# Half of the down projection's columns by Strassen's seven products, in a tuned encoder block

## The chip, the cores and the metric

The kernel runs on one core of a Trainium2 chip. Its time is the device time of one execution in microseconds, the median of a few runs; beside it stands one profiled execution. The engines are TensorE (PE; PEld is its load of the stationary operand), VectorE (DVE), ScalarE (ACT), GpSimd (POOL), and SyncE (SP), which here issues the DMAs. A matmul multiplies a stationary block (at most 128x128) by moving columns (at most 512) into a bank of PSUM, of which there are eight.

## The reference

One layer of an encoder on 256 tokens and 16 meta tokens, width 2048, all in float32. What matters here is its last part:

```python
def conv_glu(x, w_gate, w_up, conv_w, conv_b, w_down):
    g = x @ w_gate                     # 2048 -> 5632
    u = x @ w_up
    ...
    return (jax.nn.silu(gc) * u) @ w_down      # 5632 -> 2048

mix = jnp.concatenate([rmsnorm(out_a, ...), rmsnorm(out_b, ...)], axis=-1)
h = h + mix @ w_out[l]
h = h + conv_glu(rmsnorm(h, ffn_norm_g[l]), w_gate[l], w_up[l], conv_w[l], conv_b[l], w_down[l])
return h[:, N_META:]                   # (1, 256, 2048)
```

Ahead of it stand the input projection and two groups of attention heads, which the change leaves alone.

## The kernel before

**Layout and precision.** Activations are kept transposed, features on the 128 partitions and tokens along the free axis. Each float32 operand is split into two values of TensorE's rounded float32 type, hi (a copy by ACT) and lo (the value minus hi, by DVE). A product is made of three matmuls: hi by hi, hi by lo, lo by hi. The weights are the stationary operand. Where a tile holds hi and lo of the activations side by side (256 tokens each), `mm2` does the block in two matmuls: the weight's hi by 512 moving columns (L1433), the weight's lo by the 256 of hi (L1434). The two halves of the bank are added when it is evacuated. `mm3` (L398 to L400) takes three of 256 to 272 columns.

**Weights.** They come as parts of 128x1024 (eight blocks) or less. The list `pieces` sets the order in which they are loaded into five `raw` buffers, split by `split_hi` and `split_lo` into three buffers `whi` and three `wlo` (ACT L215, DVE L219, 512 columns at a time), and used by TensorE. A part's hi and lo buffers come free when TensorE is through with it.

**Stages.** Attention; output projection `w_out`; per pair of row chunks g (22 of them) the gate and up projections with their gating (`gated`), which leaves `act[:, f]`, 128 features of the 5632 with hi and lo; then the down projection: for each of the 16 output chunks m, 44 blocks f, `mm2` for the first 15 and `mm3` for the last, evacuated by `down_out` with the residual `hT[m]`, stored to `outT`.

**What sets the order.** The kernel is written as threads of steps. A planner, `Flow`, gives each step a cost and always records next the step that can start first. So the order on each engine's queue is fixed when the program is built, by those costs; on the chip every queue runs in this order, and a semaphore holds an instruction (and all behind it on its engine) until what it needs is there. The DMA issues on SP are ordered in the same way. `split_hi` and `split_lo` come ahead of other steps only when fewer than two parts are ready.

Of the kernel before, what the change touches and what calls it, by code (L numbers as in the profile page):

```python
# [15 lines left out]
P = 128  # L16
# [19 lines left out]
FC = D_FF // P  # L36

# [145 lines left out]
def encoder_block(ctx: ExitStack, tc: tile.TileContext, io):  # L183
# [101 lines left out]
    his = Slots(tiles(wpool, 3, [P, PW], "whi", F32R))  # L285
    los = Slots(tiles(wpool, 3, [P, PW], "wlo", F32R))
# [8 lines left out]

    pieces = []

# [30 lines left out]
    for m in range(KC):  # L328
        add(io["w_down"][m])

# [12 lines left out]
    def load_piece():  # L343
        p = pieces[n_loads[0]]
        n_loads[0] += 1
        p.raw = yield from one(raws)
        yield "sp", 600
        load(p.raw[:, : p.n], p.src, p.loaded, nc.sync)

# [17 lines left out]
    def split_lo():  # L367
        for p in pieces:
            p.lo = yield from one(los)
            for t, ev, ready in zip(p.parts, p.half, p.ready):  # L370
                yield ev
                yield from TT(p.lo[:, t], p.raw[:, t], p.hi[:, t].bitcast(F32), ALU.subtract)
                fl.set(ready)
            n_split[1] += 1
            fl.put(raws, p.raw)
# [38 lines left out]
    def const(name, n=P):  # L414
# [6 lines left out]
        t[:, :, :L] for t in tiles(hpool, KC, [P, 2, HW], "hl", F32R)  # L421
    ]

# [840 lines left out]

    def project(tiles, n, slots=acc):
# [10 lines left out]
    def attention_weights():  # L1276
# [74 lines left out]
        for parts, evs, evac in ((ob, ev_ob, out_b), (oa, ev_oa, out_a)):  # L1351
            for g in range(8):
# [7 lines left out]
                for c in range(2):  # L1360
                    fl.spawn(evac(2 * g + c, pss[c]))
        fl.spawn(scale_h())
# [6 lines left out]
    act = mts = None  # L1369

    def mlp_buffers():

        nonlocal act, mts
        yield ev_s2
        actx.close()
        mpool = ctx.enter_context(tc.tile_pool(name="mpool", bufs=1))
        act = mpool.tile([P, FC, 2, SEQ], F32R, name="act")
        mts = Slots(tiles(mpool, 6, [P, NT], "mt"))
# [4 lines left out]
    def gated(f, gate, up):  # L1383
# [27 lines left out]
        fl.put(mts, gc)  # L1411
        fl.set(ev_act[f])

    def down_out(m, ps):
        o = yield from one(mts)
        o_ = o[:, :SEQ]
        yield from TT(o_, ps[:, :SEQ], hT[m][:, :SEQ], ALU.add)
        if m < KC - 1:
            yield from TT(o_, ps[:, SEQ:], o_, ALU.add)
        fl.put(acc, ps)  # L1420
# [19 lines left out]
    def mlp_weights():  # L1440
        for g in range(FC // 2):
            pss = []
            for which, mul in enumerate((mm_gate, mm_up)):
                for _ in range(2):
                    pss.append((yield from one(acc)))
                for k in range(KC):
                    for c in range(2):
                        yield from mul(pss[2 * which + c], k)
            for c in range(2):
                fl.spawn(gated(2 * g + c, pss[c], pss[2 + c]))  # L1450
        for m in range(KC):
            ps = yield from one(acc)
            for f in range(FC):
                yield ev_act[f]
                if m < KC - 1:
# [5 lines left out]
            fl.spawn(down_out(m, ps))  # L1461
# [40 lines left out]
def _layout(inputs):  # L1502
# [42 lines left out]
    out["w_down"] = _columns(L0["w_down"], FC, 1)  # L1545
# [76 lines left out]
```

## Time and profile before

| what | value |
|---|---|
| time, median of 3 runs | 1132.37 us (1132.12 to 1132.48) |
| the profiled execution | 1132.44 us, of which the trace's span is 1130.7 |
| TensorE busy | 1125.1 us |
| VectorE busy | 809.6 us |
| ScalarE busy | 660.3 us |
| GpSimd busy | 122.2 us |
| moved by DMA | 203.62 MB, 180 GB/s over the span |

The span is the time from the trace's first to its last record. Busy time is the time in which an engine has at least one instruction under way. Matmuls overlap in the records, so that TensorE's pace is read from the distance between the starts of two of them.

### The profile page before, as it was taken

Reading aid. Unit: us, or ns where it says so; the run is one execution under the profiler, and the core shown is the slowest. Engines: PE = TensorE matmul, PEld = TensorE weight load, DVE = VectorE, ACT = ScalarE, POOL = GpSimd, SP = SyncE. Lnnn points to the kernel's source line nnn. Section 1 sums busy time; section 2 is a strip of 40 time slices with the busy share of each in tenths; the row PEclk is TensorE's granted clock in tenths of the full one; section 3 lists DMA queues with packets and bytes.
Section 4 is the critical chain, followed back from the end, with each engine's and each line's share of the span. In section 5 each row is a group of like instructions: output and inputs, shape, how many; then the busy total and the mean of one; then the engine's idle time right before and its main releaser. Section 6 shows DMA issues by size and latency. Waiting matters only on the chain.

```text
span 1130.7 us, 21889 instructions
## 1 busy us (share of the span) xinstructions
PE 1125.1 (100%) x8072; PEld 1062.2 (94%) x8072; DVE 809.6 (72%) x1685; ACT 660.3 (58%) x1466; POOL 122.2 (11%) x198
## 2 busy tenths in 40 slices
PE   9999999999999999999999999999999999999998
PEld 9999999999999999999999999999999888888888
DVE  8888888888878867766777677766776655555553
ACT  8787879797646655555555555555555544444442
POOL 0010212121332200100010001000100000000000
PEclk9999999999999999999999999999999999999999
DMA  9453534344655555555555555555555666676662
GB/s 347 152 171 114 163 128 142 129 145 148 208 187 185 185 186 188 177 192 186 188 177 191 185 189 181 187 187 187 185 186 187 181 195 192 208 209 197 192 196 72
DMA packets 62627, 203.62 MB, mean 180 GB/s; under 512 B 6840, under 2 KB 11448, under 8 KB 62520
## 3 DMA queue, kind: packets, MB, share of 16 engines
q1 hardware_dynamic: 62232, 201.97, 55.4%
q8 instruction: 63, 1.03, 0.4%
q14 instruction: 44, 0.36, 0.1%
q10 hardware_dynamic: 288, 0.26, 0.1%
HBM read 200.10 MB, written 2.10 MB: 179 GB/s over the span
## 4 chain that ended last, share of the span: by engine, by line
PE 97%; ACT 2%; DMA 0%; DVE 0%; POOL 0%; issue 0%; SPq 0%; POOLq 0%
PE bank L1433 28%; PE bank L398 16%; PE bank L399 16%; PE bank L400 16%; PE bank L1434 14%; PE bank L255 4%; PE bank L261 2%; ACT whi L215 1%; ACT scr L215 1%; DMA pt<-in_xT 0%; ACT bank L215 0%; ACT mq L215 0%; DVE scr L227 0%; ACT qraw L215 0%; POOL sq8r L243 0%
## 5 line engine op out<-in xcount | busy, mean ns | idle before, releaser
L219 DVE TENSOR_TENSOR wlo<-raw,whi 128x512 fp32r<-128x512 f32 (+1 forms) x737 | 512.5, 705 | 263.7 <-ACT whi L215 260.8
L215 ACT ACTIVATE whi<-raw 128x512 fp32r<-128x512 f32 (+1 forms) x737 | 459.0, 629 | 399.5 <-PE bank L1433 182.4
L398 PE MATMUL bank<-hl,whi 128*128 128x258 f32 (+1 forms) x1232 | 355.9, 289 | 0.2
L399 PE MATMUL bank<-hl,whi 128*128 128x258 f32 (+1 forms) x1232 | 351.2, 285 | 0.2 <-DVE hl L227 0.2
L400 PE MATMUL bank<-hl,wlo 128*128 128x258 f32 (+1 forms) x1232 | 349.2, 283 | 0.0
L1433 PE MATMUL bank<-hl,whi 128*128 128x512 f32 x704 | 246.3, 392 | 0.0
L400 PEld LDWEIGHTS bank<-hl,wlo 128*128 128x128 f32 x1232 | 234.9, 191 | 0.1
L399 PEld LDWEIGHTS bank<-hl,whi 128*128 128x128 f32 x1232 | 233.8, 190 | 0.7 <-DVE hl L227 0.3
L398 PEld LDWEIGHTS bank<-hl,whi 128*128 128x128 f32 x1232 | 232.4, 189 | 1.9 <-ACT whi L215 0.4
L1433 PE MATMUL bank<-act,whi 128*128 128x512 f32 x660 | 228.8, 391 | 0.0
L1434 PE MATMUL bank<-hl,wlo 128*128 128x256 f32 x704 | 197.5, 281 | 0.0
L1434 PE MATMUL bank<-act,wlo 128*128 128x256 f32 x660 | 184.8, 280 | 0.0
L1433 PEld LDWEIGHTS bank<-hl,whi 128*128 128x128 f32 x704 | 132.0, 188 | 28.9
L1433 PEld LDWEIGHTS bank<-act,whi 128*128 128x128 f32 x660 | 123.4, 187 | 27.1
L1434 PEld LDWEIGHTS bank<-hl,wlo 128*128 128x128 f32 x704 | 132.7, 188 | 0.0
L1434 PEld LDWEIGHTS bank<-act,wlo 128*128 128x128 f32 x660 | 124.7, 189 | 0.0
L243 POOL TENSOR_TENSOR mt<-mt,s 128x256 f32<-128x256 f32 x44 | 41.5, 964 | 459.6 <-ACT mt L215 459.6
L227 DVE SCALAR_TENSOR_TENSOR mt<-mt,vecs,mt 128x256 f32<-128x256 f32 x88 | 40.2, 478 | 0.0
L398 PE MATMUL bank<-ob,whi 128*128 128x258 f32 x128 | 36.8, 288 | 0.0
L399 PE MATMUL bank<-ob,whi 128*128 128x258 f32 x128 | 36.5, 285 | 0.0
L400 PE MATMUL bank<-ob,wlo 128*128 128x258 f32 x128 | 36.1, 282 | 0.0
L215 ACT ACTIVATE scr<-scr 128x272 f32<-128x272 f32 x68 | 28.1, 425 | 4.5 <-DVE scr L227 4.0
(211 smaller groups left out, 1207.8 us busy)
## 6 DMA issues: line engine op xcount, KB each, us to landing
raw<-in_w_gate SPq DMA_DIRECT2D x88, 512.0 KB, 4.4
raw<-in_w_up SPq DMA_DIRECT2D x88, 512.0 KB, 4.5
raw<-in_w_down SPq DMA_DIRECT2D x80, 512.0 KB, 4.4
raw<-in_w_in SPq DMA_DIRECT2D x54, 512.0 KB, 3.9
raw<-in_w_out SPq DMA_DIRECT2D x32, 512.0 KB, 4.0
raw<-in_w_down SPq DMA_DIRECT2D x16, 256.0 KB, 3.4
raw<-in_w_cq SPq DMA_DIRECT2D x5, 512.0 KB, 6.1
bias<-in_na_bias SPq DMA_DIRECT2D x8, 272.0 KB, 4.5
```

Source lines behind the costliest of these rows:

```text
L215: nc.scalar.activation(out, in_, f, **kw)
L219: nc.vector.tensor_tensor(out, a, b, op)
L227: nc.vector.scalar_tensor_tensor(out, a, s, b, op0, op1)
L243: nc.gpsimd.tensor_tensor(out, a, b, op)
L255: nc.tensor.matmul(o, l, r, start=start, stop=stop)
L261: nc.tensor.transpose(o, i, ident[:n, :n])
L398: nc.tensor.matmul(ps, whi, xhi, start=start, stop=False)
L399: nc.tensor.matmul(ps, whi, xlo, start=False, stop=False)
L400: nc.tensor.matmul(ps, wlo, xhi, start=False, stop=stop)
L1433: nc.tensor.matmul(ps, whi, x, start=start, stop=False)
L1434: nc.tensor.matmul(ps[:, :n], wlo, x[:, 0, :], start=False, stop=stop)
```

## The change

**Which columns.** The first 1024 of the 2048 output columns are no longer computed in the transposed layout but as tokens by columns, by Strassen's scheme (the variant with seven products and sums that are used again): the activations are cut in halves of 128 tokens and, per row pair g, of 128 features (chunks 2g and 2g+1); the weights of the pair in halves of 128 rows and 512 columns. Each product is 128 tokens by 512 columns, with the activations as the stationary and the weights as the moving operand, as three matmuls (hi by hi, hi by lo, lo by hi). Seven banks of PSUM collect the seven products over the 22 row pairs. The other 1024 columns stay on the plain path, in one bank.

**Sums of the activations.** `value_sums` makes four 128x128 sums per pair after the gating, splits them and stores them to DRAM; `load_pair` brings them back in the down stage (tiles `sin`).

**Sums of the weights.** A pair's four weight quarters are loaded as 1 MB into one of two `quarters` tiles; `weight_sums` makes three sums on DVE, one 1024 and two 512 wide. The four parts of a pair, A (1024 columns: two quarters), B (512: one quarter), C and D (1024 each: two sums each), are split into hi and lo like other parts; 3584 columns are split per pair, where the plain path would split 2048. The tiles take the space of `hl`, which comes free at the end of the last up projection.

**Order.** Parts of the scheme and of the plain chunks alternate: three plain parts, then two scheme parts and one plain, four scheme parts where a new plain chunk begins, and eight plain parts at the end.

**Around it.** The residual of the first eight chunks is transposed on TensorE after the output projection (`residual_transposed`, 16 transposes). `scheme_out` combines the seven products after the last pair, adds the residual on POOL and stores to `out`. `down_out` of the plain chunks evacuates by two copies on ACT, adds the residual on POOL and the second half on DVE. There are four instead of three buffers `whi` and `wlo`, and a smaller reserve for DMA descriptors of POOL, which starts no DMAs here.

The diff, cut to its core:

```diff
+SF = 1024
+ST = SF // P
+AHEAD, BEHIND = 3, 8
...
     raws = Slots(tiles(wpool, 5, [P, PW], "raw"))
-    his = Slots(tiles(wpool, 3, [P, PW], "whi", F32R))
-    los = Slots(tiles(wpool, 3, [P, PW], "wlo", F32R))
+    his = Slots(tiles(wpool, 4, [P, PW], "whi", F32R))
+    los = Slots(tiles(wpool, 4, [P, PW], "wlo", F32R))
...
+    scheme = [(r, p) for r in row_pairs for p in r.pieces]
+    n = len(others) - BEHIND
+    down += others[:AHEAD]
+    for i in range(AHEAD, n):
+        k = 4 if others[i - 1][0] != others[i][0] else 2
+        down += scheme[:k] + [others[i]]
+        del scheme[:k]
+    down += scheme + others[n:]
...
+    def load_pair(r):
+        r.raw = yield from one(quarters)
+        t = r.raw
+        for i in range(2):
+            yield "sp", 600
+            ev = r.loaded if i else Event()
+            load(t[:, i * PW : (i + 1) * PW], io["w_down_s"][r.g][:, i * PW : (i + 1) * PW], ev, nc.sync)
...
+        r.S = yield from one(s_parts)
+        yield s_saved[r.g]
+        yield "sp", 600
+        load(r.S, s_dram[r.g], r.ev_S, nc.sync)
+        fl.spawn(weight_sums(r), 2)
...
+    def weight_sums(r):
+        yield r.loaded
+        r.sums = yield from one(sums4)
+        t, raw, h = r.sums, r.raw, PW // 2
+        yield from TT(t[:, :PW], raw[:, h : 3 * h], raw[:, :PW], ALU.subtract)
...
+        yield from TT(t[:, PW : PW + h], raw[:, PW : PW + h], t[:, :h], ALU.subtract)
+        yield from TT(t[:, PW + h :], t[:, PW : PW + h], raw[:, PW + h :], ALU.subtract)
...
+    def residual_transposed():
+        for i in range(ST // 2):
+            for c in range(2):
+                yield ev_sqh[2 * i + c]
+            pt = yield from one(tps)
+            yield from TR(
+                [(pt[:, (2 * t + c) * P : (2 * t + c + 1) * P], hT[2 * i + c][:, t * P : (t + 1) * P])
+                 for t in range(2) for c in range(2)]
+            )
...
+    def value_sums(g, a, b):
...
+        yield from TT(S[0], A21, A22, ALU.add)
+        yield from TT(S[1], S[0], A11, ALU.subtract)
+        yield from TT(S[2], A11, A21, ALU.subtract)
+        yield from TT(S[3], A12, S[1], ALU.subtract)
...
+        yield from split_plain(parts[:, : PW // 2], parts[:, PW // 2 :], s)
+        yield "sp", 600
+        load(s_dram[g], parts.bitcast(F32), s_saved[g], nc.sync)
...
+        if m < KC - ST - 1:
+            t = yield from one(mts)
+            yield from ACT(o_, ps[:, :SEQ], AF.Copy)
+            yield from ACT(t[:, :SEQ], ps[:, SEQ:], AF.Copy)
+            fl.put(acc, ps)
+            yield from PTT(o_, o_, hT[ST + m][:, :SEQ], ALU.add)
+            yield from TT(o_, t[:, :SEQ], o_, ALU.add)
...
+    PRODUCTS = {"A": (3, 2), "B": (1,), "C": (5, 7), "D": (6, 4)}
...
+    def scheme_products(p, r):
...
+            yield from block()
+            t = slice(i * PW // 2, (i + 1) * PW // 2)
+            first, last = f == 0, f == FC - 2
+            yield from MM(
+                product3(sums7[n], a, (p.hi[:, t], p.lo[:, t]), first, last)
+            )
...
+    def scheme_out():
...
+        yield from ACT(c1, sums7[1], AF.Copy)
+        fl.put(acc, sums7[1])
+        yield from TT(C[0][0], sums7[2], c1, ALU.add)
...
-    nc = _bacc.Bacc("TRN2", target_bir_lowering=False, num_devices=1)
+    nc = _bacc.Bacc("TRN2", target_bir_lowering=False, num_devices=1, dynamic_dma_scratch_size=1024)
```

How it moves DVE's queue, at a place in the middle of the down projection. Before, `wlo` are the lo parts of the weights, and `mt` with `res` is an evacuation of a chunk with its residual:

```order
L219 TENSOR_TENSOR wlo_89<-raw_80,whi_86 128x512 x2
L219 TENSOR_TENSOR wlo_90<-raw_81,whi_87 128x512 x2
L219 TENSOR_TENSOR wlo_88<-raw_82,whi_85 128x512
L219 TENSOR_TENSOR wlo_89<-raw_83,whi_86 128x512 x2
L219 TENSOR_TENSOR wlo_90<-raw_84,whi_87 128x512 x2
L219 TENSOR_TENSOR mt_5198<-bank_72,res_3966 128x256
L219 TENSOR_TENSOR wlo_88<-raw_80,whi_85 128x512
L219 TENSOR_TENSOR mt_5198<-bank_72,mt_5198 128x256
```

Now, on the same engine and stage; L231 is the same helper. A `quarters` tile that is written is a pair's tile of weight sums, and `wlo` that reads one is a split of a scheme part:

```order
L231 TENSOR_TENSOR wlo_92<-quarters_10215,whi_88 128x512 x2
L231 TENSOR_TENSOR quarters_10191<-quarters_10141 128x1024
L231 TENSOR_TENSOR wlo_89<-quarters_10215,whi_85 128x512 x2
L231 TENSOR_TENSOR wlo_90<-raw_80,whi_86 128x512 x2
L231 TENSOR_TENSOR mt_5230<-mt_5231,mt_5230 128x256
L231 TENSOR_TENSOR wlo_91<-quarters_10141,whi_87 128x512 x2
L231 TENSOR_TENSOR wlo_92<-quarters_10141,whi_88 128x512
L231 TENSOR_TENSOR wlo_89<-raw_81,whi_85 128x512 x2
L231 TENSOR_TENSOR quarters_10191<-quarters_10141,quarters_10191 128x512
L231 TENSOR_TENSOR quarters_10191<-quarters_10191,quarters_10141 128x512
L231 TENSOR_TENSOR wlo_90<-quarters_10191,whi_86 128x512 x2
L231 TENSOR_TENSOR wlo_91<-quarters_10191,whi_87 128x512 x2
```

Between two plain parts there now stand splits of scheme parts and weight sums; the first sum of the next pair stands ahead of the split of this pair's D.

The queue of SP in the same stage, before, with what each issue waits for (DMAHW are the DMAs issued earlier):

```order
L338 DMA raw_82<-in_w_down 128x1024 [waits DMAHW7_49,DMAHW1_49,DVE_49]
L338 DMA raw_83<-in_w_down 128x1024 [waits DMAHW2_49,DVE_49]
L338 DMA raw_84<-in_w_down 128x1024 [waits DMAHW3_49,DVE_49]
L338 DMA raw_80<-in_w_down 128x1024 [waits DMAHW4_49,DVE_49]
L338 DMA raw_81<-in_w_down 128x512 [waits DMAHW5_49,DVE_49]
L1422 DMA outT<-mt_5199 128x256 [waits DVE_49]
```

Now, where `sin` is the load of a pair's activation sums and `quarters` that of its weights:

```order
L391 DMA raw_84<-in_w_down 128x1024 [waits DMAHW3_49]
L391 DMA quarters_10166<-in_w_down_s 128x1024 [waits DMAHW4_49,Activation_49]
L391 DMA quarters_10166<-in_w_down_s 128x1024 [waits DMAHW5_49]
L391 DMA sin_5241<-s_dram_114 128x1024 [waits DMAHW6_49,PE_49]
L391 DMA raw_80<-in_w_down 128x1024 [waits DMAHW7_49]
L391 DMA raw_81<-in_w_down 128x512 [waits DMAHW0_49,Activation_49]
L391 DMA quarters_10141<-in_w_down_s 128x1024 [waits DMAHW1_49,DVE_49]
L391 DMA quarters_10141<-in_w_down_s 128x1024 [waits DMAHW2_49,DVE_49]
L391 DMA sin_5240<-s_dram_115 128x1024 [waits DMAHW3_49,PE_49]
```

The weight loads now share the queue with loads of quarters, which wait for DVE and ACT, and with loads of activation sums, which wait for TensorE.

## Rows read from the trace of the kernel before

**Rows 1.** The page's parts 1 and 2: busy times, and TensorE by slices.
```profile
span 1130.7 us, 21889 instructions
PE 1125.1 (100%) x8072; PEld 1062.2 (94%) x8072; DVE 809.6 (72%) x1685; ACT 660.3 (58%) x1466; POOL 122.2 (11%) x198
...
PE   9999999999999999999999999999999999999998
...
PEclk9999999999999999999999999999999999999999
```

**Rows 2.** Busy time by stretch: early, gate and up, down.
```profile
core 0: us, PE busy (x) PEld busy (x) DVE busy (x) ACT busy (x) POOL busy (x), PEclk, DMA share, GB/s
10.00:15.00 5.00, 5.00 (x42) 4.91 (x41) 4.64 (x10) 4.45 (x11) 0.00 (x0) 1.00 1.04 416
...
30.00:40.00 10.00, 10.00 (x81) 10.00 (x81) 9.72 (x23) 7.26 (x18) 0.00 (x0) 1.00 0.42 134
395.00:883.00 488.00, 488.00 (x3424) 458.27 (x3423) 343.47 (x685) 255.52 (x471) 39.60 (x42) 1.00 0.57 185
885.00:1111.00 226.00, 226.00 (x1306) 199.27 (x1305) 123.46 (x200) 102.75 (x168) 1.90 (x2) 1.00 0.65 198
```

**Rows 3.** Groups from 880 to 1130 us: count, busy us, mean ns, idle before.
```profile
L1433 PE MATMUL bank<-act,whi 128*128 128x512 f32 x660 | 228.8, 391 | 0.0
L1434 PE MATMUL bank<-act,wlo 128*128 128x256 f32 x660 | 184.8, 280 | 0.0
```

**Rows 4.** Timeline of PE, down projection's first blocks and last chunk: start, length.
```profile
882.56 0.39 PE L1433 MATMUL bank<-act,whi 128*128 128x512 f32 x1
882.79 0.28 PE L1434 MATMUL bank<-act,wlo 128*128 128x256 f32 x1
882.90 0.39 PE L1433 MATMUL bank<-act,whi 128*128 128x512 f32 x1
...
1111.36 0.28 PE L398 MATMUL bank<-act,whi 128*128 128x256 f32 x1
...
1127.06 0.28 PE L400 MATMUL bank<-act,wlo 128*128 128x256 f32 x1
```

**Rows 5.** Timeline of PE in attention: six transposes (L261) and what follows.
```profile
229.54 0.82 PE L261 MATMUL bank<-consts,p 128*128 128x128 f32 x6
230.12 0.36 PE L398 MATMUL bank<-late,whi 128*128 128x258 f32 x1
230.32 0.28 PE L399 MATMUL bank<-late,whi 128*128 128x258 f32 x1
230.43 0.29 PE L400 MATMUL bank<-late,wlo 128*128 128x258 f32 x1
```

**Rows 6.** Timelines of POOL (first row) and DVE beside and behind it.
```profile
886.43 1.90 POOL L243 TENSOR_TENSOR mt<-mt,s 128x256 f32<-128x256 f32 x2 [20.72 <-ACT mt L215]
...
887.00 0.72 DVE L219 TENSOR_TENSOR wlo<-raw,whi 128x512 fp32r<-128x512 f32 x1
887.64 0.41 DVE L219 TENSOR_TENSOR mt<-bank,mt 128x256 f32<-128x256 f32 x1
...
888.52 1.28 DVE L219 TENSOR_TENSOR wlo<-raw,whi 128x512 fp32r<-128x512 f32 x2
889.73 0.41 DVE L219 TENSOR_TENSOR act<-mt,act 128x256 fp32r<-128x256 f32 x1
890.07 0.41 DVE L219 TENSOR_TENSOR mt<-mt,mt 128x256 f32<-128x256 f32 x1
```

**Rows 7.** DMA issues (count, KB, us to landing), and SP's longest wait (total, times, longest).
```profile
raw<-in_w_down SPq DMA_DIRECT2D x80, 512.0 KB, 4.4
...
SPq L338 <- DVE wlo L219: 767.2, 316, 6.7
```

**Rows 8.** Waits of TensorE's weight loads for a weight part (total, times, longest).
```profile
PEld bank L398 <- ACT whi L215: 0.4, 1, 0.4
```

More of the change, by code (lines that the diff above doesn't have):

```diff
@@ L294, in __init__, with release, used @@
             self.ready = [Event() for _ in self.parts]
+        def release(self):
+            fl.put(raws, self.raw)
+    class Quarters(Piece):
+        def __init__(self, pair, which):
+            super().__init__(None, PW if which != "B" else PW // 2)
+            self.pair, self.which = pair, which
+        def release(self):
+            if self.which in "AB":
+                self.pair.used()
+            elif self.which == "D":
+                fl.put(sums4, self.pair.sums)
+    class RowPair:
+        def __init__(self, g):
+            self.g, self.loaded, self.ev_S, self.left = g, Event(), Event(), 3
+            self.pieces = [Quarters(self, which) for which in "ABCD"]
+        def used(self):
+            self.left -= 1
+            if self.left == 0:
+                fl.put(quarters, self.raw)
     pieces = []
+    row_pairs = [RowPair(g) for g in range(FC // 2)]
     def add(src):
@@ L345, in load_piece @@
         n_loads[0] += 1
+        if isinstance(p, Quarters):
+            if p.which == "A":
+                yield from load_pair(p.pair)
+            return
         p.raw = yield from one(raws)
@@ L1262, in scale_h @@
         fl.set(ev_s2)
+    res = [None] * (ST // 2)
+    ev_resT = Event()
+    def residual_transposed():
[7 more added lines that the diff above has]
+            )
+            res[i] = hpool.tile([P, 2, 2 * P], F32, tag=f"late{i}", name=f"resT{i}")
+            yield from ACT(res[i], pt.rearrange("p (t c) -> p t c", t=2), AF.Copy)
+            fl.put(tps, pt)
+        fl.set(ev_resT)
     def project(tiles, n, slots=acc):
@@ L1448, in mlp_weights @@
                         yield from mul(pss[2 * which + c], k)
+                    if g == FC // 2 - 1 and which and k % 4 == 3:
+                        hl_free(k // 4)
             for c in range(2):
                 fl.spawn(gated(2 * g + c, pss[c], pss[2 + c]))
-        for m in range(KC):
-            ps = yield from one(acc)
-            for f in range(FC):
+        f = 0
+        for which, p in down:
+            if isinstance(p, Quarters):
+                yield from scheme_products(p, p.pair)
+                continue
+            if f == 0:
+                ps = yield from one(acc)
+            for _ in range(p.n // P):
                 yield ev_act[f]
-                if m < KC - 1:
+                if which < KC - ST - 1:
                     yield from mm2(ps, act[:, f], SEQ, f == 0, f == FC - 1)
```

127 lines of the change are left out of this document (111 added, 16 removed).

## The prediction

> **What bounds the kernel now.** I read the page first, then the busy times by stretch, then the groups of the last stretch, then single starts on TensorE. [rows 1]: TensorE (PE) is busy for 1125.1 of 1130.7 us, in every slice, at a granted clock of 1.00, the 2.4 GHz level ([rows 2]). Busy says little, since the records of pipelined matmuls overlap ([rows 3]: 660 of 391 ns and 660 of 280 ns would fill 443 us, and the stretch has 250); what counts is the distance from one start to the next. [rows 4]: the down projection's first matmul starts at 882.56, the last chunk's first at 1111.36: 15 chunks x 44 blocks in 228.80 us, 346.7 ns per block of two matmuls, without a hole. So a TensorE column taken out of this stretch shortens the kernel, as long as the engines that feed it keep up. How much they have left: [rows 2] gives VectorE (DVE) 123.46 of 226 us (55%) and ScalarE (ACT) 102.75 in the down projection, DVE 343.47 of 488 (70%) in gate and up. The span is 1130.7 and the profiled execution 1132.44, so 1.74 lie outside; the median of 1132.37 is the same within 0.01%.
>
> **What the change takes from TensorE.** 8 of the 16 output chunks leave the plain path: 8 x 44 = 352 blocks x 346.7 ns = **122.0 us**. In their place each of 22 row pairs gives 7 products x 3 matmuls, 462 matmuls with 512 moving columns. No row shows such matmuls in a row; the nearest is the first matmul of a block, also 512 wide, which holds TensorE for 0.23 (882.56 to 882.79, [rows 4]). Ends: the block less a 256-wide matmul at the last chunk's pace (15.70 us for 131 of them, 0.120) leaves 0.227; the block less the 0.11 to the next start leaves 0.237. I take 0.230: **106.3 us** (104.9 to 109.5). Gain 15.7. Seven products instead of eight are 12.5% of 122; the rest is that two matmuls per block become fewer, longer ones.
>
> **What it adds to TensorE.** Four groups of four 128x128 transposes of the residual after the output projection. [rows 5]: six take 0.58 (229.54 to 230.12) and the matmul behind them 0.20 where its successors take 0.12: (4 x 0.097 + 0.08) x 4 = **1.9 us**, all on the path, since nothing there waits. What they read, h of the first 8 chunks, is finished while the output projection still runs on the other 8, so TensorE does not wait for it.
>
> **What it adds beside TensorE, at nothing, and under which cover.** (1) Gate and up: per row pair four sums of 128x128 (at most the 0.34 of a 256-wide operation, 889.73 to 890.07 [rows 6]) and one 512-wide split (0.605: two in 1.21, 888.52 to 889.73), 22 x 1.97 = 43 us of DVE, which goes from 70% to 79%. Cover: 22.2 us of TensorE per pair. The store to DRAM waits on the SP queue for that split; behind it stand the next weight loads, whose parts are needed only after the four split and five loaded parts ahead of them, 8 blocks each, over 20 us of TensorE. If that cover went, each pair would cost what its sums take, 2 us. (2) The tail: after the last product TensorE still has 12 plain blocks and the last chunk, 12 x 0.347 + 15.8 = 20 us. The combination of the seven sums needs there one ACT copy, seven 512-wide DVE operations (4.2 us) and eight POOL additions (0.95 each by the two in 1.90, [rows 6]: 7.6), then four stores; even end to end that is 12.5 us plus a landing. Uncovered it would be those 12.5. What follows the last matmul stays as it is. (3) The fourth buffer for hi and lo. Waiting for a split cost TensorE's weight loads 0.4 us in one place [rows 8], and 5.6 us of the span is all that TensorE is not busy, start and end included. I take 0; ends 0 and -1.
>
> **The stretch on which it hangs.** Between the first and the last product TensorE has 106.3 + 37 plain parts of 272 blocks (94.3) = 200.6 us. DVE has there, per pair, seven 512-wide splits (A two, B one, C two, D two) and the three weight sums, one 1024 wide and two 512 wide; and 68 splits of the plain parts and 6 evacuations of 256. The 1024-wide operation is in no row: at most two 512-wide ones (1.21), at least 0.605 + 2 x 0.265 = 1.135 by the step from 256 to 512; I take 1.15. Sum: 222 x 0.605 + 22 x (1.15 + 1.21) + 6 x 0.34 = 134.3 + 51.9 + 2.0 = **188.2 us, 94% of TensorE's time**. Can DVE run so full with TensorE fed? [rows 2]: from 30 to 40 us it was busy 9.72 of 10 us and TensorE 10.00 with 81 matmuls. ACT has 222 splits of about 0.6 there, two thirds. DMA moves 22 x 1.57 MB + 17.8 MB = 52.4 MB, 261 GB/s, against 198 now and 416 from 10 to 15 us. So DVE is the second limit by 12.4 us, 0.56 us per pair.
>
> That slack is not evenly spread. Where a plain chunk ends, four scheme parts stand in a row (C, D and the next A, B): DVE needs 7 x 0.605 + 2.36 = 6.6 us while TensorE has 21 x 0.23 = 4.8, a deficit of 1.8; between two plain parts DVE gains 0.65 per half pair back. The four split parts ahead, 5 to 7 us of TensorE, carry that. The tightest place is the first two pairs, which meet the last group's gating and value sums on DVE (order of DVE's queue: some 21 us of work from the first weight sum to the third pair's, while TensorE has 22 until the second pair's C): there the margin is below 1 us, and I allow **1 us** of waiting (0 to 3).
>
> **Sum.** 1132.44 - 122.0 + 106.3 + 1.9 + 1.0 = 1119.6; with the ends of the 512-wide matmul (-1.4, +3.2), the buffer (-1) and the waiting (-1, +2): 1116.2 to 1124.8.
>
> A rule of the pages speaks against the change, and here is the row first. [rows 6]: while POOL ran its two additions (886.43 to 888.33), a 512-wide split of two SBUF operands held DVE from 887.00 to 887.64, 0.64 instead of 0.605. The Trainium skill, page "SBUF — State Buffer", section "Who interferes with whom", says that a DVE instruction with two SBUF inputs contends with a GpSimd instruction that reads SBUF, and that the second fully blocks until the first has finished. By that rule each of the six POOL additions that the change puts into the stretch could hold DVE for its 0.95, 5.7 us of the 12.4; the row shows 0.035 for one. It belongs to the first rival.
>
> **The rivals.** *DVE falls behind a little.* Its queue is in order, and each pair's weight sums stand in it ahead of splits that are ready, waiting for a 1 MB load of quarters. For it: the wait is new, the load shares SP's queue with loads that wait for TensorE, and the six POOL additions are in the stretch too. Against it: about 9 us of DVE work lie between the last use of a quarters tile and the next sums in it, and 512 KB land in 4.4 us [rows 7]. With 0.8 us lost per pair DVE needs 188.2 + 17.6 = 205.8, 5.2 more than TensorE: 1118.6 + 5.2 = **1123.8**; the case runs from 1122 to 1129.
>
> *DVE's wait for the quarters becomes the bound; slower than before.* The quarters of pair g+1 are issued on SP behind the load of pair g's value sums, and that waits until TensorE has done pair g-2's D. What is then let go at once is 0.5 + 0.8 + 1.05 = 2.4 MB: 6 us at 416 GB/s, 12 at the 198 of this stretch. In the second case DVE's in-order queue stands still for 3 us per pair. It breaks even with the kernel before when a pair loses (13.8 + 12.4) / 22 = 1.2 us; at 1.5 us DVE needs 221.2, and the time is 1118.6 + 20.6 = **1139**. Against it: 198 GB/s is no limit of the transfers; SP's queue spent 767.2 us waiting for DVE to free buffers [rows 7].
>
> *Nothing measurable.* The same wait at 1.0 to 1.3 us per pair: within 0.2% of 1132.4, which is about what a measurement of this kernel can tell from no change. *Better than the sum.* 512-wide matmuls at 0.227 without any waiting and a shorter start by the fourth buffer: **1115.5**. *That it does not do what it says*: the plain path would keep its 660 blocks; the built order has seven products of three per pair, so this has no chance of its own.
>
> **How the numbers follow.** Forecast, 1116 to 1122: 0.57, time 1119.6. A little behind, 1122 to 1129: 0.26. Better, below 1116: 0.06. Nothing measurable: 0.05. Slower: 0.06. Range 1116 to 1128, which leaves out 0.06 below and 0.13 above. Faster by over 0.2% (below 1130.1): 0.57 + 0.26 + 0.06 = 0.89.
>
> **What would show it.** In the profile after: the first plain block at about 884.5 (1.9 later than 882.56); from there to the last chunk's first matmul 228.8 - 14.7 = 214 us; starts of products 0.23 apart; DVE between the first and last product about 94% busy, with waits for quarters loads well below 0.5 us per pair; the POOL additions next to splits of 0.6 to 0.65. Wrong would be: products more than 0.24 apart (the term of the matmuls), holes before products whose last releaser is a split (first rival), holes of over 1 us whose chain goes through a weight sum to a quarters load (second), or a down stretch with little gain and TensorE dense (more work left on it than counted).

## The result, and the profile of the changed kernel

The changed kernel takes 1121.79 us (1121.53 to 1121.96), beside 1132.38 (1132.12 to 1132.48) for the kernel before: ratio 0.9907, with a 95% interval of 0.9889 to 0.9924. The forecast was 1119.6 with a range of 1116 to 1128, so the sign and the size are right and the time is 2.2 us above the likeliest value. The profiled execution took 1121.53.

Parts 1 and 2 of the page, to be laid beside [rows 1]:

```profile
span 1119.7 us, 21894 instructions
...
PE 1113.9 (99%) x7846; PEld 1043.8 (93%) x7846; DVE 912.5 (81%) x1911; ACT 714.8 (64%) x1573; POOL 150.1 (13%) x213
...
PE   9999999999999999999999999999999999999998
...
DVE  8888888888877777777777777777777899999995
...
PEclk9999999999999999999999999999999999999999
```

TensorE is as dense as before, at the same granted clock; VectorE has gained 103 us of work and is nearly full in the seven slices of nines, which hold the products; the last slice is the end of the kernel. The busy times by stretch answer to [rows 2] (columns as there): gate and up, the first plain blocks, and the stretch from the first product to the last.

```profile
core 0: us, PE busy (x) PEld busy (x) DVE busy (x) ACT busy (x) POOL busy (x), PEclk, DMA share, GB/s
395.00:885.00 490.00, 490.00 (x3440) 460.25 (x3439) 372.05 (x787) 267.40 (x493) 39.60 (x42) 1.00 0.64 209
885.23:893.55 8.32, 8.32 (x50) 7.34 (x49) 8.29 (x20) 4.63 (x10) 1.82 (x2) 1.00 0.86 331
893.55:1096.20 202.65, 202.65 (x1008) 169.85 (x1007) 193.92 (x300) 138.35 (x236) 6.41 (x6) 1.00 0.73 257
```

Gate and up: DVE 76% (forecast 79%), TensorE without a hole. Between the products: 202.65 us of TensorE (forecast 200.6) beside 193.92 of DVE (forecast 188.2), 95.7% of the stretch, and 257 GB/s (forecast 261).

Single starts on TensorE, which answer to [rows 4]: the last plain blocks ahead of the first product (L1583, L1584), products (L267), the plain blocks behind them, and the last chunk (L485).

```profile
885.23 0.39 PE L1583 MATMUL bank<-act,whi 128*128 128x512 f32 x1
...
893.21 0.39 PE L1583 MATMUL bank<-act,whi 128*128 128x512 f32 x1
893.44 0.28 PE L1584 MATMUL bank<-act,wlo 128*128 128x256 f32 x1
893.55 0.39 PE L267 MATMUL bank<-whi,sin 128*128 128x512 f32 x1
893.78 0.40 PE L267 MATMUL bank<-wlo,sin 128*128 128x512 f32 x1
...
950.30 0.39 PE L1583 MATMUL bank<-act,whi 128*128 128x512 f32 x1
...
952.77 0.40 PE L1583 MATMUL bank<-act,whi 128*128 128x512 f32 x1
...
1100.45 0.28 PE L485 MATMUL bank<-act,whi 128*128 128x256 f32 x1
```

Products start 0.23 apart, as forecast. From the first plain block to the last chunk it is 1100.45 - 885.23 = 215.22 us, against 228.80 before and 214 in the forecast. Two things were not forecast. The first block starts at 885.23, 2.67 later than 882.56 where 1.9 was expected. And the plain blocks behind the first product are slower: 7 blocks from 950.30 to 952.77, 352 ns each, where the 24 blocks ahead of the first product (885.23 to 893.55) take 346.7 as before. Over all 272 blocks between the products it is 351.3 ns.

Waits between the first and the last product (total, times, longest):

```profile
DVE wlo L231 <- ACT whi L227: 6.3, 11, 1.5
...
DVE mt L231 <- POOL mt L255: 0.6, 1, 0.6
DVE quarters L231 <- DMA quarters<-in_w_down_s: 0.6, 1, 0.6
...
PEld bank L267 <- DVE wlo L231: 0.4, 1, 0.4
```

DVE waited for a load of quarters once, for 0.6 us, in 22 pairs, although these loads land later than [rows 7] has them (page, DMA issues: KB each, median us to landing):

```profile
quarters<-in_w_down_s SPq DMA_DIRECT2D x44, 512.0 KB, 7.0
raw<-in_w_down SPq DMA_DIRECT2D x40, 512.0 KB, 5.5
```

TensorE waited for a split in one place only, near 916.5, at the products of the third pair's C and D: the tight start that the prediction named, one pair further on.

### The profile page after: what moved, and what is told of

It is laid out like the page before. It is cut to its first block, busy times and chain, and to the rows that moved or that the text cites. A ratio compares the mean times of both kernels' runs of the same rounds, so it can differ in the third digit from the quotient of the medians.

```text
span 1119.7 us, 21894 instructions
## 1 busy us (share of the span) xinstructions
PE 1113.9 (99%) x7846; PEld 1043.8 (93%) x7846; DVE 912.5 (81%) x1911; ACT 714.8 (64%) x1573; POOL 150.1 (13%) x213
## 4 chain that ended last, share of the span: by engine, by line
PE 94%; ACT 3%; DVE 2%; issue 1%
PE bank L1583 21%; PE bank L485 16%; PE bank L486 16%; PE bank L487 16%; PE bank L267 13%; PE bank L1584 11%; PE bank L273 2%; ACT whi L227 1%; ACT scr L227 1%; DVE scr L239 1%; DVE wlo L231 1%; ACT qraw L227 0%; PE bank L563 0%; ACT nav L227 0%; ACT bank L227 0%
## 5 line engine op out<-in xcount | busy, mean ns | idle before, releaser
L227 ACT ACTIVATE whi<-raw 128x512 fp32r<-128x512 f32 (+1 forms) x649 | 402.0, 629 | 271.2 <-PE bank L1583 115.6
L231 DVE TENSOR_TENSOR wlo<-raw,whi 128x512 fp32r<-128x512 f32 (+1 forms) x649 | 446.2, 701 | 130.8 <-ACT whi L227 127.6
L485 PE MATMUL bank<-hl,whi 128*128 128x258 f32 (+1 forms) x1232 | 356.0, 289 | 0.0
L1583 PE MATMUL bank<-hl,whi 128*128 128x512 f32 x704 | 246.3, 392 | 0.0
L485 PEld LDWEIGHTS bank<-hl,whi 128*128 128x128 f32 x1232 | 232.7, 189 | 1.5 <-ACT whi L227 0.3
L1584 PE MATMUL bank<-hl,wlo 128*128 128x256 f32 x704 | 197.5, 281 | 0.0
L1583 PEld LDWEIGHTS bank<-hl,whi 128*128 128x128 f32 x704 | 132.0, 188 | 28.9
L1584 PEld LDWEIGHTS bank<-hl,wlo 128*128 128x128 f32 x704 | 132.7, 188 | 0.0
L227 ACT ACTIVATE whi<-quarters 128x512 fp32r<-128x512 f32 x154 | 95.9, 631 | 54.9 <-PE bank L1583 35.7
L1583 PE MATMUL bank<-act,whi 128*128 128x512 f32 x308 | 109.9, 397 | 0.0
L255 POOL TENSOR_TENSOR mt<-mt,s 128x256 f32<-128x256 f32 x44 | 41.4, 961 | 461.6 <-ACT mt L227 461.6
L231 DVE TENSOR_TENSOR wlo<-quarters,whi 128x512 fp32r<-128x512 f32 x154 | 99.3, 691 | 3.6 <-ACT whi L227 3.2
L1584 PE MATMUL bank<-act,wlo 128*128 128x256 f32 x308 | 86.4, 280 | 0.0
L1583 PEld LDWEIGHTS bank<-act,whi 128*128 128x128 f32 x308 | 57.8, 188 | 13.8
L267 PE MATMUL bank<-whi,sin 128*128 128x512 f32 x176 | 62.5, 396 | 0.0
L1584 PEld LDWEIGHTS bank<-act,wlo 128*128 128x128 f32 x308 | 58.1, 189 | 1.6
L267 PE MATMUL bank<-whi,act 128*128 128x512 f32 x132 | 48.3, 393 | 0.0
L267 PEld LDWEIGHTS bank<-whi,sin 128*128 128x128 f32 x176 | 33.0, 188 | 7.9
```

Source lines behind the costliest of these rows:

```text
L227: nc.scalar.activation(out, in_, f, **kw)
L231: nc.vector.tensor_tensor(out, a, b, op)
L255: nc.gpsimd.tensor_tensor(out, a, b, op)
L267: nc.tensor.matmul(o, l, r, start=start, stop=stop)
L485: nc.tensor.matmul(ps, whi, xhi, start=start, stop=False)
L1583: nc.tensor.matmul(ps, whi, x, start=start, stop=False)
```

## The experiments

The theory after this reading: TensorE still sets the time; DVE is the second limit, some 9 us behind it; what is missing to the forecast lies outside the products, in attention and in the plain blocks. The rivals: DVE at 96% already costs part of the time, or the fourth buffer brings nothing that is worth its price.

### The fourth buffer, alone, taken away, and given late

**The kernel before with four buffers**, without the scheme:

```
-    his = Slots(tiles(wpool, 3, [P, PW], "whi", F32R))
-    los = Slots(tiles(wpool, 3, [P, PW], "wlo", F32R))
+    his = Slots(tiles(wpool, 4, [P, PW], "whi", F32R))
+    los = Slots(tiles(wpool, 4, [P, PW], "wlo", F32R))
...
-    nc = _bacc.Bacc("TRN2", target_bir_lowering=False, num_devices=1)
+    nc = _bacc.Bacc("TRN2", target_bir_lowering=False, num_devices=1, dynamic_dma_scratch_size=1024)
```

> The kernel before, with the fourth buffers for hi and lo alone (and the smaller reserve that makes room for them). Its order on every engine through attention is that of the changed kernel, which reaches the output projection 0.9 us later than the kernel before. Theory: the other order in attention, which the fourth buffer brings, costs those 0.9 us: about 1133.3 us, TensorE's first block of the down projection at about 883.5 instead of 882.56. Rival: the buffer is harmless, and the 0.9 us come from another part of the change (tiles of hl grouped by four, other addresses): 1132.4, first block at 882.6. Rival of the prediction, which put it at 0 to -1: 1131.4 to 1132.4.

Measured: 1134.12 (1133.84 to 1134.42), ratio 1.0015 (1.0006 to 1.0025). The direction is as expected, the size twice that. The down projection takes its 228.79 us as before; all of the loss is ahead of gate and up.

**The changed kernel with three buffers:** the first four lines above in reverse.

> The changed kernel with three buffers for hi and lo instead of four. Theory: attention runs as before (0.9 us back), but three parts split ahead, 4 to 5 us of TensorE, carry DVE's deficits of 1.8 us where four scheme parts stand in a row less well: holes of 1 to 5 us in sum before products, 1122 to 1126 in all. Rival, the fourth buffer is not needed at all: 1120.9. Rival, it is what makes the change possible: above 1130.

Measured: 1123.31 (1122.07 to 1123.71). Attention is back to its pace of before, but the down projection takes 218.38 instead of 215.22, with 14 holes on TensorE, 3.8 us together. Two of them (timeline of PE; in brackets the idle time ahead of the row and what ended it):

```profile
913.28 0.39 PE L1584 MATMUL bank<-act,wlo 128*128 128x256 f32 x1 [0.83 <-DVE wlo L231]
...
990.25 0.38 PE L1584 MATMUL bank<-act,wlo 128*128 128x256 f32 x1 [0.99 <-DVE wlo L231]
```

With one part less of lookahead, TensorE meets the uneven places of DVE's queue. So the buffer has a price in attention and a gain in the down projection, and the two can be had apart:

**The fourth buffer handed to the planner only at the gate and up stage:**

```
-    his = Slots(tiles(wpool, 4, [P, PW], "whi", F32R))
-    los = Slots(tiles(wpool, 4, [P, PW], "wlo", F32R))
+    whis, wlos = tiles(wpool, 4, [P, PW], "whi", F32R), tiles(wpool, 4, [P, PW], "wlo", F32R)
+    his, los = Slots(whis[:3]), Slots(wlos[:3])
...
+        fl.put(his, whis[3])
+        fl.put(los, wlos[3])
```

> The changed kernel, in which the fourth buffers for hi and lo are given to the planner only when the gate and up stage begins, so that attention keeps the order of the kernel before. Theory: 0.9 us back, 1120.9 us, first block of the down projection at about 884.4 instead of 885.23 (the transposes' 1.8 remain); the down stretch unchanged at 215.2. Rival, the 0.9 us do not come from the order: 1121.8 and 885.2.

Measured: 1121.05 (1120.99 to 1121.39), faster than the changed kernel by 0.7. The start is earlier as expected, by 0.97; the down projection is not quite unchanged, 215.58 with a wait of 0.6 near 916, so not all of it arrives. The first gate and up matmul (timeline of PE) in the kernel before, in the one with four buffers alone, in the changed kernel and in this one:

```profile
394.15 0.40 PE L1433 MATMUL bank<-hl,whi 128*128 128x512 f32 x1
```
```profile
395.91 0.39 PE L1433 MATMUL bank<-hl,whi 128*128 128x512 f32 x1
```
```profile
396.81 0.39 PE L1583 MATMUL bank<-hl,whi 128*128 128x512 f32 x1
```
```profile
395.84 0.39 PE L1585 MATMUL bank<-hl,whi 128*128 128x512 f32 x1
```

The last has the transposes and not the early buffer: +1.7 us are the transposes. The third has both: +2.66, so the buffer costs 1.0 there; in the kernel before it costs 1.76. The transposes can also be read by themselves, in the changed kernel: a group of four (`res`) holds TensorE for 0.35, and the matmul behind it for 0.20 where its successors take 0.12, which is 0.43 a group and 1.7 in all.

```profile
383.04 0.60 PE L273 MATMUL bank<-consts,res 128*128 128x128 f32 x4
383.39 0.37 PE L485 MATMUL bank<-hl,whi 128*128 128x258 f32 x1
383.59 0.28 PE L486 MATMUL bank<-hl,whi 128*128 128x258 f32 x1
```

What TensorE does last before the output projection's first block (`ob`) shows how: in the changed kernel (first fence) it is another order than with the late buffer (second).

```profile
286.53 0.60 PE L267 MATMUL bank<-sum_b,consts 128*128 128x258 f32 x2
286.78 0.47 PE L485 MATMUL bank<-ob,whi 128*128 128x258 f32 x1
```
```profile
284.85 0.39 PE L267 MATMUL bank<-nak,qs 128*4 128x16 f32 x6
285.09 0.37 PE L485 MATMUL bank<-ob,whi 128*128 128x258 f32 x1
```

The planner records what can start first. With a free buffer it splits weights earlier, and the attention's small steps fall elsewhere in the queues.

That the buffer costs 1.76 us in one kernel and 1.0 in the other is in part the scatter of single executions. The same first block of `ob` in the kernel before, with the late buffer and a later start of the products (the next experiment), with four buffers alone, and in a kernel that runs the changed kernel's order (two more weight sums, below):

```profile
285.16 0.37 PE L398 MATMUL bank<-ob,whi 128*128 128x258 f32 x1
```
```profile
284.70 0.37 PE L485 MATMUL bank<-ob,whi 128*128 128x258 f32 x1
```
```profile
287.27 0.47 PE L398 MATMUL bank<-ob,whi 128*128 128x258 f32 x1
```
```profile
287.58 0.47 PE L486 MATMUL bank<-ob,whi 128*128 128x258 f32 x1
```

All twelve kernels here have one of two orders up to this block, alike on every engine and on SP: the four with three buffers in attention reach it at 284.70 to 285.16, the eight with four at 286.78 (the changed kernel) to 287.58. So the early buffer costs attention between 1.6 and 2.9 us, and kernels of the same order lie up to 0.8 apart. On the way from there to gate and up the early order is shorter, by 0.3 without the transposes (108.64 against 108.99) and by 0.7 with them (110.03 against 110.75); why is open. What is left by gate and up is 1.0 in the changed kernel's execution, one of the two earliest of its order, and up to 1.8 in the others with the scheme.

**The late buffer, and the first product one plain part later** (`AHEAD, BEHIND = 4, 7` in place of `3, 8`):

> The kernel with the late fourth buffer, and the first product one plain part (8 blocks) later in the down projection, the last one a part later. Theory: the only waiting left in that kernel (0.6 us near 915 us, where the first pairs meet the last group's gating) goes: 1120.5 us instead of 1121.05. Rival: the hole moves along with the products, or the tail behind the last product, now with 4 plain blocks and the last chunk (17 us), no longer covers the combination of the seven sums: 1121 to 1124.

Measured: 1120.28 (1120.07 to 1120.59), ratio 0.9894 (0.9877 to 0.9911): the fastest of the kernels here that compute the whole result. No hole is left in the down projection (214.89 us, against 215.58 with the late buffer alone), and from the last chunk's first matmul to the end of the span it is 19.24 us, as in the changed kernel (19.25), so 4 plain blocks and the last chunk still cover the combination of the sums. In the profiled execution gate and up also starts 0.4 earlier (395.45); the order ahead of it is that of the late buffer on every engine, so this is scatter, and 0.7 is what the later start of the products brings.

### How far DVE is from being the bound

**Without the weight sums.** The three sums per pair are left out, and the splits read the loaded quarters instead, which stay held until D is split:

```
-        yield from TT(t[:, :PW], raw[:, h : 3 * h], raw[:, :PW], ALU.subtract)
...
-        c.raw, d.raw = t[:, :PW], t[:, PW:]
+        c.raw, d.raw = raw[:, :PW], raw[:, PW:]
...
-        yield from TT(t[:, PW : PW + h], raw[:, PW : PW + h], t[:, :h], ALU.subtract)
-        yield from TT(t[:, PW + h :], t[:, PW : PW + h], raw[:, PW + h :], ALU.subtract)
```

> The changed kernel without the three weight sums of each pair: C and D are split from the loaded quarters themselves, which leaves out part of the computation. DVE has 52 us less in the stretch between the products, some 70% instead of 96%. Theory A, DVE's load slows the plain blocks: between the products a block takes 346.7 ns again instead of 351.3, the holes (0.5 us) vanish: 1.8 us less, 1120.0. Theory B, the blocks' pace is set by what TensorE itself ran before them, not by DVE: 351 ns remain, only the holes vanish: 1121.3. Rival, DVE is already the limit in places: over 3 us less, below 1119.

Measured: 1121.53 (1121.39 to 1122.01), which overlaps the changed kernel's runs. Busy times between its products:

```profile
893.74:1096.00 202.26, 202.26 (x1008) 169.83 (x1007) 151.88 (x234) 139.22 (x236) 5.55 (x6) 1.00 0.74 260
```

42 us less on DVE save 0.4 us on TensorE, the waiting near 916.5. (52 were expected; a split that no other follows at once counts 0.68 us instead of 0.60, and more of them now stand alone.) So DVE's 96% costs next to nothing in the changed kernel, and the plain blocks' slower pace, 351.3 ns here too, is not DVE's doing.

**One sum more, two sums more.** The last sum of each pair is computed twice, or three times:

```
-        yield from TT(t[:, PW + h :], t[:, PW : PW + h], raw[:, PW + h :], ALU.subtract)
+        for _ in range(2):
+            yield from TT(t[:, PW + h :], t[:, PW : PW + h], raw[:, PW + h :], ALU.subtract)
```

> The changed kernel with the last of the three weight sums of each pair computed twice: 22 more 512-wide operations on DVE between the first and the last product, 22 x 0.605 = 13.3 us. The profile of the changed kernel has DVE busy for 193.9 of 202.65 us there, so with 207.2 DVE has more to do than TensorE. Theory (DVE is the second limit, a few per cent behind TensorE, and the prediction's sum of the two engines is right): 207.2 - 202.65 = 4.6 us are added, 1126.4 us; down projection 219.8 us from its first block to the last chunk instead of 215.2, holes on TensorE that end on a split of DVE. Rival (DVE's busy share has slack in it, since an operation that waits for POOL or for a buffer counts as busy): 1122 us, no holes.

> The changed kernel with the last weight sum of each pair computed three times: 26.6 us more on DVE between the first and the last product, 220.5 us against TensorE's 202.65. Theory (DVE takes the place of TensorE as the bound, and from there every operation on DVE is paid in full): +17.9, 1139.7 us, that is 13.3 more than with one more sum. Rival (slack in DVE's busy time): about 1130.

Measured: 1127.02 (1126.43 to 1127.20) and 1141.30 (1140.63 to 1142.07), ratios 0.9953 (0.9937 to 0.9970) and 1.0081 (1.0066 to 1.0096). The sum of each column of busy times between the products (length, then PE, PEld, DVE, ACT, POOL), one more and two more:

```profile
sum 207.97, PE 204.37 PEld 169.19 DVE 206.35 ACT 132.96 POOL 9.27; mean PE 204.37 PEld 169.19 DVE 206.35 ACT 132.96 POOL 9.27
```
```profile
sum 221.78, PE 207.63 PEld 171.38 DVE 219.45 ACT 129.37 POOL 11.54; mean PE 207.63 PEld 171.38 DVE 219.45 ACT 129.37 POOL 11.54
```

DVE is now busy for 99% of both stretches, TensorE for 98% and 94%, and TensorE's waits end on DVE (longest holes of the two kernels, timeline of PE):

```profile
919.51 0.50 PE L267 MATMUL bank<-wlo,sin 128*128 128x512 f32 x1 [1.72 <-DVE wlo L231]
```
```profile
951.80 0.50 PE L267 MATMUL bank<-wlo,sin 128*128 128x512 f32 x1 [2.62 <-DVE wlo L231]
```

The first 13 us on DVE cost 5.2, the second 14.3 (13.8 in this stretch; for the rest attention, in the same order, ended 0.6 later in this execution). That is the picture of two engines in parallel: the slack of 9 us is real, and beyond it each operation is paid in full. Two operations of 0.6 us per pair turn this gain into a loss.

The second kernel shows one thing more. Behind two of its holes, 1.83 us before 912.15 and the 2.62 at 951.80, TensorE's granted clock was lower for some microseconds, in the row shown 0.50, the 1.2 GHz level (columns as in [rows 2]):

```profile
954.00:956.00 2.00, 2.00 (x8) 1.71 (x7) 2.00 (x5) 0.89 (x2) 0.00 (x0) 0.50 1.02 416
```

The products from 912.62 to 915.18 stand 0.43 apart instead of 0.23. It was back at 1.00 from 916 and from 958. Holes as long near 1022 and 1093 left it at 1.00, and so did the 1.72 at 919.51 in the kernel with one more sum. DVE stayed full meanwhile, so little of it can be in the 13.8; how much is not shown.

**Six products.** Product 1 is left out in 20 of 22 pairs; its splits stay:

```
-            yield from MM(
-                product3(sums7[n], a, (p.hi[:, t], p.lo[:, t]), first, last)
-            )
+            if n != 1 or first or last:
+                yield from MM(
+                    product3(sums7[n], a, (p.hi[:, t], p.lo[:, t]), first, last)
+                )
```

> The changed kernel with product 1 left out in 20 of the 22 pairs (so one of the sums is not complete); its splits on ACT and DVE stay. TensorE loses 20 x 3 x 0.231 = 13.9 us of its 202.65 and would need 188.8 between the first and the last product; DVE is busy for 193.9 of them. Theory (DVE is the next limit, 8.7 us behind): 1113 us or a little more, with holes on TensorE of 5 us or more whose releaser is a split on DVE. Rival (DVE keeps up, TensorE alone sets the time): 1107.7 us, no holes.

Measured: 1112.60 (1112.43 to 1112.91). Between its products:

```profile
sum 193.62, PE 191.82 PEld 157.43 DVE 191.37 ACT 132.80 POOL 18.91; mean PE 191.82 PEld 157.43 DVE 191.37 ACT 132.80 POOL 18.91
```

Of 13.9 us taken from TensorE 9.2 arrive; the stretch is as long as DVE's work, and 29 holes with 5.4 us stand on TensorE. A further saving on TensorE in this stretch would have to take work off DVE too.

### What the seventh-for-eighth saving is worth

**Eight products.** Product 1 is computed twice per pair:

```
-    PRODUCTS = {"A": (3, 2), "B": (1,), "C": (5, 7), "D": (6, 4)}
+    PRODUCTS = {"A": (3, 2), "B": (1, 1), "C": (5, 7), "D": (6, 4)}
...
+            again = p.which == "B" and i == 1
+            t = slice(0, PW // 2) if again else slice(i * PW // 2, (i + 1) * PW // 2)
...
```

> The changed kernel with product 1 of every pair computed a second time into the same sum (the sum is then not the reference's): eight products of three matmuls per pair in place of seven, as a plain product of halves would need, and no change on DVE. Theory (TensorE sets the time, 0.231 us per 512-wide matmul): 22 x 3 x 0.231 = 15.2 us are added, less the 0.4 us of waiting that the extra work covers: 1136.6 us, so that the new path without the seventh-for-eighth saving would be slower than the plain path (1132.4). Rival (part of the changed kernel's time is DVE's pace, so that extra TensorE work hides beside it): 1130 to 1134.

Measured: 1136.44 (1136.22 to 1136.88), ratio 1.0038 (1.0025 to 1.0051). The stretch grows from 202.65 to 217.33, without a hole: 14.7 us for 66 matmuls, 0.222 each, or 0.227 with the 0.3 us of waiting that they cover. With eight products the new path is slower than the plain one: 528 x 0.231 = 122.0 for the matmuls is what 352 plain blocks cost, and the transposes, the buffer and the slower plain blocks come on top. All of the gain is the product that Strassen's scheme saves.

### The pace of the plain blocks

**One pair, then thirteen plain parts.** The remaining 21 pairs come later and closer together:

```
         k = 4 if others[i - 1][0] != others[i][0] else 2
+        if AHEAD + 2 <= i < AHEAD + 14:
+            k = 0
```

> The changed kernel with the first pair's products where they are, then 13 plain parts in a row without any product, and the other 21 pairs closer together at the end of the stretch. Only the pace of the plain blocks is read from it: in the changed kernel a block takes 346.7 ns before the first product and 351.3 ns after it. Theory A (what TensorE ran before sets it, and it stays so until TensorE waits for something): all blocks of the 13 parts take 351.3 ns. Theory B (it is the work that runs beside them: splits of scheme parts, loads of quarters): back to 346.7 ns within the 13 parts. The time as a whole goes up, since 21 pairs in less room are more than DVE can feed: about 1128 us.

Measured: 1134.09 in one run, 6 more than expected. The pace: timeline of PE in the stretch of 37 us that holds no product.

```profile
908.03 0.40 PE L1585 MATMUL bank<-act,whi 128*128 128x512 f32 x1
...
925.05 0.50 PE L1585 MATMUL bank<-act,whi 128*128 128x512 f32 x1 [1.67 <-ACT mt L227]
...
925.51 0.39 PE L1585 MATMUL bank<-act,whi 128*128 128x512 f32 x1
...
938.58 0.40 PE L1585 MATMUL bank<-act,whi 128*128 128x512 f32 x1
```

37 blocks from 925.51 to 938.58 take 353 ns each, 24 us and more after the last product and 14 us or less before the next. So the pace is not set by what runs beside the blocks at that moment; it stays as the first products left it. The second half of that theory does not hold as it stands: two waits of 1.7 us, as at 925.05, did not bring 346.7 back. It does come back elsewhere: in the kernel with two sums more, six runs of eight blocks (from 902.17, 923.10, 933.54, 994.24, 1024.21 and 1075.69) took about 347 each, while most took 351 to 352. Four of the six begin within 1.3 us behind a wait of TensorE in front of a product, and so does the run from 917.65 with the late buffer; but other such waits changed nothing. Kernels without a hole between the products (without weight sums, eight products, the later start) have no such run. What in TensorE's stream differs stays open.

The time missed because of those two waits, among others: seven banks are held by the products' sums, so where one plain chunk follows another directly, TensorE waits until ACT has emptied the one bank left. In the changed kernel the four scheme parts that stand at each change of chunk leave time for this, and no such wait is seen there. The others come at the end, where 159 products' matmuls in a row stand 0.285 apart, since DVE can't feed them faster.

## Why the prediction was right, step by step

| step | predicted, us | measured, us | from |
|---|---|---|---|
| 352 plain blocks removed | -122.0 | -122.0 | pace of before, taken and not measured again |
| 462 product matmuls | +106.3 | +106.8 | 202.65 less 272 blocks (95.55) and 0.3 of waiting |
| transposes | +1.9 | +1.7 | start of gate and up with the late buffer |
| fourth buffer | 0 | +1.0 | the same start, changed kernel |
| pace of the remaining plain blocks | not in the sum | +1.3 | 272 x 4.6 ns, 12 x 5.8 |
| waiting for splits | +1.0 | +0.3 | holes near 916.5 |
| sum | -12.8 | -10.9 | |

1132.44 - 10.9 = 1121.5, the time of the profiled execution. It closes because the rows are read from the two profiled executions themselves; the row of the buffer alone could be up to 0.8 larger in another one of the same order, and in part the misses cancel. The mechanism was the forecast's own: TensorE bounds, gains by longer and fewer columns, and DVE keeps up with a margin.

**The bound and the main terms.** The 0.230 for a 512-wide matmul, taken from the first half of a block [rows 4], holds: 106.8 / 462 = 0.231. Runs of 21 go at 0.228, runs of 9 and 12 between plain parts at 0.232 to 0.233, so the change of kind has a small price.

**What failed: two terms at nothing.** For the fourth buffer, "I take 0; ends 0 and -1" looked only at who waits for a split [rows 8]. The buffer acts through the planner, which orders all of attention anew: +1.0 here and up to 1.8 in other executions of the same order, outside both ends. An end above nothing was missing, as for any change of a resource by which a program is ordered. And the remaining plain blocks were taken at the pace of before, +1.3; no row of before could show that. With 0.5 more for the products, and 0.7 of waiting and 0.2 of transposes that did not come, that is the 1.9 us between the sum and the run.

**DVE's 188.2 was 193.9.** Two parts of the sum were too small. Splits in a row stand 0.60 apart, but one that no other operation follows at once counts its 0.68, and some beside POOL take longer: from start to start, or to the end where DVE then idles, 0.622 on average, 138.7 instead of 134.3 for the splits of the stretch. And 2.1 us of the last group's gating and value sums lie behind the first product, which the sum left out. The weight sums go the other way. Each reads the result of the one before, and then one takes longer; but the first pair's stand ahead of the first product, so that 21 and not 22 pairs' lie in the stretch (timeline of DVE; group of the 1024-wide sums in the stretch, with count, busy us, mean ns and idle before):

```profile
1012.93 1.40 DVE L231 TENSOR_TENSOR quarters<-quarters,quarters 128x512 f32<-128x512 f32 x2
1014.25 2.49 DVE L231 TENSOR_TENSOR wlo<-quarters,whi 128x512 fp32r<-128x512 f32 x4
...
L231 DVE TENSOR_TENSOR quarters<-quarters 128x1024 f32<-128x1024 f32 x21 | 25.6, 1217 | 0.6 <-DMA quarters<-in_w_down_s 0.6
```

From the first start to the next row's it is 1.32 for two: 0.71 from the first sum to the second, which reads it, and 0.61 on to the split, where four splits take 0.60 each. With 1.16 for the wide one a pair's sums take 2.44 instead of 2.36; 21 pairs make 51.2 instead of 51.9. None of this reached the time, because the slack was 12 us by the forecast and 9 in fact. That it was a slack, and that DVE can run 99% full, the kernels with more sums showed.

**The rivals.** *DVE a little behind* did not happen: 0.4 us of waiting. One more 512-wide operation per pair would have made it so: 1127.0, in that rival's span. *The wait for quarters* came once, 0.6 us: the loads land after 7.0 us instead of 4.4, but the wait shows that two `quarters` tiles were enough for that; one tile was not tried. *Slower* needed some 20 us more on DVE, the slack of 9 and the gain of 10.6; with 26.6 more it came, at 1141.3. *Better* was added up wrongly: 0.227 per matmul, no waiting and the shorter start by the buffer make 1119.6 - 1.4 - 1.0 - 1.0 = 1116.2, the forecast's own lower end, and not 1115.5.

**GpSimd's additions.** Timelines of POOL (L255) and DVE in the changed kernel, two places:

```profile
908.66 2.28 POOL L255 TENSOR_TENSOR mt<-mt,res 128x256 f32<-128x256 f32 x1 [16.98 <-ACT mt L227]
941.67 0.73 POOL L255 TENSOR_TENSOR mt<-mt,res 128x256 f32<-128x256 f32 x1 [30.73 <-ACT mt L227]
```
```profile
906.05 4.29 DVE L231 TENSOR_TENSOR wlo<-quarters,whi 128x512 fp32r<-128x512 f32 x7
910.98 0.43 DVE L231 TENSOR_TENSOR mt<-mt,mt 128x256 f32<-128x256 f32 x1 [0.63 <-POOL mt L255]
...
940.68 1.22 DVE L231 TENSOR_TENSOR quarters<-quarters 128x1024 f32<-128x1024 f32 x1
941.82 1.73 DVE L231 TENSOR_TENSOR wlo<-quarters,whi 128x512 fp32r<-128x512 f32 x2
```

At 908.66 DVE was in a row of splits, kept its 0.60 each, and the addition took 2.28 instead of 0.73. At 941.67 the addition came ahead of the splits, and two of them took 1.73 instead of 1.28: DVE lost 0.45. Of six additions three were of this kind; two more left DVE's splits within 0.1 us. The 0.035 of [rows 6] was the lucky case, and "splits of 0.6 to 0.65" was wrong beside three of them. The Trainium skill, page "SBUF — State Buffer", section "Who interferes with whom", says that the one of the two that issues second is held; the addition at 908.66 and the splits at 941.82 agree on who is held. The addition at 941.67 does not show it: a weight sum of two SBUF operands was still running (940.68 to 941.90), and the addition took 0.73, where the shortest of the six took 0.72. The price to DVE, some 2 us with the wait at 910.98, was below the 5.7 that the rule could have made of it. All of it fell into DVE's slack, except perhaps the 0.4 near 916.5.

## What to carry to other kernels

Count the second engine as closely as the first: here 13.6 us saved on TensorE brought a full second engine to within 9 us of the bound, and one more cheap operation per step would have eaten half the gain, two all of it. Where a planner orders the program by free buffers, an added buffer is a new order everywhere: give it only to the stage that needs it, and price it from both sides. A scheme with fewer products pays only when its products are priced against the real cost of the path it replaces: with eight of them, this path would have lost.

## What was not expected of the hardware

- The same block of two matmuls, 512 and 256 wide, takes 346.7 ns or 351 to 353 at the same granted clock (1.00), and stays slow for 37 us after the 512-wide products that came before it; 42 us less work on DVE did not change it. In kernels where TensorE waited in front of products some runs went at 347 again. Its cause is open.
- A DVE operation that reads what the one before wrote starts 0.71 us behind it at 512 columns, an independent one 0.60.
- DVE ran at 99% busy for over 200 us with TensorE waiting on it; from there the added operations cost their own time and little more (13.8 us for 13.3).
- In the kernel with two sums more the granted clock fell to the 1.2 GHz level behind two of TensorE's holes of about 2 us, and not behind others as long.
